# Narrow y groups copied out of PSUM by ScalarE and scaled later by VectorE, and exponentials that stand back from the third query split on, in a two-layer decoder trunk

## The chip, the cores and the metric

The kernel runs on one core of one Trainium2 chip. The metric is the device time of one execution in microseconds (us), the median of several runs. A profile is one further execution, taken with the hardware profiler; its span reaches from the first to the last instruction.

The engines go by the profile's names. PE is the matmul engine and PEld its weight load, ACT is ScalarE, DVE is VectorE, POOL is GpSimd, SP issues most of the DMAs. PSUM is the memory that PE writes its results to, eight banks of 128 x 512 fp32; SBUF is the working memory.

## The reference

One sequence of 256 tokens, width 2048, passes a recurrent layer and an attention layer, each followed by a SwiGLU block:

```
h = rms_norm(x, g);  y_branch, x_branch = split(h @ w_in)        # recurrent block
xb = causal_depthwise_conv(x_branch);  hs = rg_lru(xb)           # gates, a scan over time
x = x + (hs * gelu(y_branch)) @ w_out
x = x + (silu(gate) * up) @ w_out2                               # SwiGLU of rms_norm(x)
k, v = split(rms_norm(x) @ w_kv)                                 # one K/V, k normed by head
q = rms_norm over each head of (rms_norm(x) @ w_q)               # 32 heads of 64, 4 K/V heads
x = x + softmax([mask(q k / 8), sink])[:-1] v @ w_o              # window of 128 tokens
x = x + (silu(gate) * up) @ w_out3
```

All of it is float32.

## The kernel before, in words

**Layout.** Features lie on the partitions, tokens on the free axis: an activation tile is 128 features x 256 tokens, and there are 16 of them. Every operand of a matmul is split into a high part, rounded by an ACT copy, and a low part, the difference, made by DVE. A product is the sum of three matmuls: high weight by high activation, high weight by low activation, low weight by high activation. An activation's two parts lie side by side in one tile of 512 columns.

**Jobs.** The weights come as 707 jobs of 512 KB. `stream` (L278) goes through them: load of job i+4 by SP, split of job i+3 into `hi` and `lo` (L264, L267), matmuls of job i (L330). A group is eight or more jobs that make four output tiles, one bank each (`group`, L347). A bank is wide when the high weight meets both parts of the activation in one matmul of 512 columns, so that two halves have to be added at the end; it is narrow when all three products are added up in 256 columns. With `sync` given, the first two of a group's four banks are wide (L368), without it all four are narrow. At the group's end `done` empties the banks; a bank is handed out again in the order in which it became free.

**The order of the background work.** All else (norms, gates, softmax) is written as generators in a list, `bg`. A job has two half-ticks, each of 12 matmuls of 256 columns. At each, `run_bg` (L203) lets the first generator of the list that is due go on, then the next, until the estimated cost of what it issued passes a budget for DVE (640 ns, later 740) or for ACT (800 ns, later 900); every call through `a`, `tt`, `stt` and `ts` adds its estimate. A plain `yield` leaves a generator due at once, `yield n` puts it off by n half-ticks. If a job's activation isn't there yet, `need` (L216) steps all generators until it is. What is issued in this order is then put in order for each engine by the compiler.

**The recurrent layer** is made in the order x0 x1 x2 g0 x3 g1 y0 g2 g3 y1 g4 g5 y2 g6 g7 y3 (L54): four x groups, eight gate jobs, four y groups. `y_group` (L716) empties its banks through `scaled` (L583), which multiplies by `rstd`, the norm's factor, on the way out of PSUM, into half tiles named h. Its task then computes the gelu, multiplies by the recurrence's result and splits the product into the tiles `zs`, which the groups of `lru_out` consume, two per job. y1 and y3 are given `SYNC`, y0 and y2 are not (L756).

**The attention layer.** Four groups of w_q make 16 tiles q, of two heads each. A group's task (L1012) squares and splits its four tiles (L1020 to L1023), then lets PE sum the squares by head (L1031), copies the sums to a half tile h (L1034), lets PE transpose it (L1039) and makes the heads' factors. `pairs()` (L946) works on the 16 tiles in visits that are three half-ticks apart: a visit issues on PE the values of one tile, the scores of a newer one and the transposes of one between. `softmax` (L910) is a part of it: two masked maxima by DVE (L918), then the Exps by ACT (L934), then a division by POOL. The flag `summing` keeps a softmax from issuing its Exps ahead of the copy L1034. `hold` keeps visits out of the last job of one w_q group and the first of the next.

Of the kernel before, what the change touches and what calls it, by code (L numbers as in the profile page):

```python
# [15 lines left out]
ALU = mybir.AluOpType  # L16
# [3 lines left out]
T = 256  # L20
# [29 lines left out]
class Trunk:  # L50
# [548 lines left out]
    def lru(self, gains, rn):  # L599
# [116 lines left out]
        def y_group(g):  # L716
            def done(ps):
                v = []
                for f in range(4):
                    o = self.half()  # L720
                    self.scaled(o, ps[f])
                    v.append(o)

                def task():
                    th = []
                    yield 1
                    for f in range(4):
                        s = self.slot(F32)
                        o = s[:, 0:T]
                        th.append((s, o))  # L730
                        self.a(o, v[f], AF.Square, scale=math.sqrt(0.044715 * GK))
                        yield
                    for f in range(4):
                        o = th[f][1]
                        self.stt(o, o, GK, v[f], ALU.add, ALU.mult)
                        self.a(o, o, AF.Tanh)
                        yield
                    for f in range(4):
                        s, o = th[f]
                        k = 4 * g + f  # L740
                        self.stt(o, o, 1.0, v[f], ALU.add, ALU.mult)
                        while not hs[k].ready:
                            yield 1
                        h = hs[k].ap[:, 0:T]
                        self.stt(o, o, 0.5, h, ALU.mult, ALU.mult)
                        yield
                        q = self.slot()
                        self.split_act(q, o)
                        self.free(s)
                        self.free(hs[k].ap)  # L750
                        self.free_half(v[f])
                        zs[k].ap = q
                        zs[k].ready = True
                        yield
                self.spawn(task())
            self.group(lambda c: w[g, c], ND, xs, done, g == 3, self.SYNC if g in (1, 3) else ())  # L756

        for step in self.ORDER.split():
# [109 lines left out]
    def attn(self, xs, r, gains, rn):  # L868
# [41 lines left out]
        def softmax(k, rr, ps, sc):  # L910
            f = k % 4
            sm = self.half()
            mx, nm, es, den = (sm[:, 4 * i:4 * i + 4] for i in range(4))
            for hh in range(2):
                for b, c0, c1 in blocks:
                    i = b * 2 + hh
                    self.dve += 69 + 1.042 * (c1 - c0)
                    nc.vector.tensor_tensor_reduce(  # L918
                        sc[hh][:, c0:c1], ps[hh][:, c0:c1], con[:, K_MASK + c0:K_MASK + c1],
                        rr[:, b * 8 + f * 2 + hh:b * 8 + f * 2 + hh + 1],  # L920
                        par[:, C_SINK + 4 * k + hh:C_SINK + 4 * k + hh + 1], ALU.add, ALU.max,
                        accum_out=mx[:, i:i + 1])
                self.free_mbank(ps[hh])
                yield
            while self.summing:
                yield 1
            self.ts(nm, mx, -1.0, None, ALU.mult)
            self.tt(es, par[:, C_SINK + 4 * k:C_SINK + 4 * k + 4], mx, ALU.subtract)
            self.a(es, es, AF.Exp)
            for hh in range(2):  # L930
                for b, c0, c1 in blocks:
                    i = b * 2 + hh
                    o = sc[hh][:, c0:c1]
                    self.a(o, o, AF.Exp, bias=nm[:, i:i + 1], accum_out=den[:, i:i + 1])  # L934
                yield
            self.tt(den, den, es, ALU.add)
            self.rcp(den, den)
            for hh in range(2):
                o = sc[hh][:, P:2 * P]
                nc.gpsimd.tensor_tensor(o, o, sc[hh][:, 2 * P:3 * P], ALU.add)  # L940
                o = sc[hh][:, 0:2 * P].rearrange("p (b q) -> p b q", b=2)
                nc.gpsimd.tensor_tensor(o, o, den[:, hh:4:2].unsqueeze(2).broadcast_to([P, 2, P]), ALU.mult)
                yield
            self.free_half(sm)

        def pairs():  # L946
# [4 lines left out]
            while n < ND or A or B or C:  # L951
# [44 lines left out]
                if new:  # L996
                    sc = [self.slot(F32) for _ in range(2)]
                    yield from softmax(new[0], new[2], ps, sc)
                    C = (new[0], sc)
# [4 lines left out]
        for g in range(4):  # L1004
            def done(ps, g=g):
                v = []
                for p in ps:
                    s = self.slot(F32)
                    self.pull(p, s[:, 0:T])
                    v.append(s)  # L1010

                def task():  # L1012
                    while not self.rv[r].ready:
                        yield 1
                    rt = self.rstd[r][:, T:T + 2]
                    if g == 0:
                        self.stt(r2, rt, 1.0 / HD, rt, ALU.mult, ALU.mult)
                    qs = []
                    for f in range(4):
                        self.a(v[f][:, T:2 * T], v[f][:, 0:T], AF.Square)  # L1020
                        qs.append(self.slot())
                        self.split_act(qs[f], v[f][:, 0:T])
                        yield  # L1023
                    self.summing = True
                    yield 1
                    while not self.room():
                        yield 1
                    p = self.mbank()

                    for f in range(4):  # L1030
                        self.pe_other(p[32 * f:32 * f + 32, 0:T], con[:, K_HS:K_HS + 32], v[f][:, T:2 * T],  # L1031
                                      start=True, stop=True)
                    h = self.half()
                    self.a(h, p[:, 0:T])  # L1034
                    self.summing = False
                    yield
                    yield 1
                    for b in range(2):
                        self.pe_other(p[:, T + b * P:T + b * P + P], h[:, b * P:b * P + P], one, f=nc.tensor.transpose)  # L1039
                    self.free_half(h)  # L1040
                    yield 1
                    rr, m, t = (self.rrs[g][:, 16 * i:16 * i + 16] for i in range(3))
                    for b in range(2):
                        self.ts(m[:, 8 * b:8 * b + 8], p[:, T + b * P:T + b * P + P:16], r2[:, b:b + 1], EPS,
                                ALU.mult, ALU.add)
                    self.free_mbank(p)
                    for q in v:
                        self.free(q)
                    self.rsqrt(rr, m, t)
                    for b in range(2):  # L1050
                        self.ts(rr[:, 8 * b:8 * b + 8], rr[:, 8 * b:8 * b + 8], rt[:, b:b + 1],
                                1.0 / math.sqrt(HD), ALU.mult, ALU.mult)
                    yield
                    for f in range(4):
                        todo.append((4 * g + f, qs[f], rr))
                    if g == 0:
                        self.spawn(pairs())
                    yield
                self.spawn(task())
            self.group(lambda c, g=g: w[g, c], ND, xs, done, g == 3, self.SYNC, packed=True)  # L1060
        self.project(self.d["w_o"], ND, at, gains, rn, late=True)
# [99 lines left out]
```

## Time and profile before

| | |
|---|---|
| runs | 1980.66, 1982.5, 1982.1 us; median 1982.1 us |
| profiled execution | 1980.68 us; span 1978.9 us |
| PE busy | 1971.8 us, 100% of the span |
| DVE busy | 1256.3 us, 63% |
| ACT busy | 1063.0 us, 54% |
| POOL busy | 70.5 us, 4% |
| granted clock of PE | 1.000 |
| DMA | 377.10 MB, mean 191 GB/s |

Busy times are shares of the span and overlap. The end of a matmul is modelled, so a busy PE can hide short waits; they are seen better in the distance from one matmul's start to the next one's. The page divides the span into 40 slices; in tenths, DVE is busy 8988876 in the first seven, that is during the recurrent layer, and 4 to 7 later; ACT 7798655 there, and 3 to 7 later.

### The profile page before, as it was taken

The numbers are of one execution on the slowest core, as the hardware profiler recorded it, in microseconds if no ns is written. First come the engines' busy times: TensorE is split into PE (matmuls) and PEld (weight loads), VectorE is DVE, ScalarE is ACT, GpSimd is POOL, SyncE is SP. The second block draws the span as 40 slices with busy tenths as digits, with TensorE's granted clock in tenths as the row PEclk, the third lists the DMA queues.
The fourth block names the chain that finished last, engine by engine and source line by source line (L and its number), as shares of the span: only waits on it lengthen the run. The fifth ranks groups of instructions, "written<-read, shape, count | busy, mean of one in ns | idle before, by whom it ended". The sixth has DMA issues, their size and how long they took to land.

```text
span 1978.9 us, 40162 instructions
## 1 busy us (share of the span) xinstructions
PE 1971.8 (100%) x16683; PEld 1930.5 (98%) x16683; DVE 1256.3 (63%) x1981; ACT 1063.0 (54%) x1606; POOL 70.5 (4%) x100
## 2 busy tenths in 40 slices
PE   9999999999999999999999999999999999999999
PEld 9999999999999999999999889999999999999999
DVE  8988876556556655545668776755655565554443
ACT  7798655444444444434556775544544454443342
POOL 0000000000000000000002461000000000000000
PEclk9999999999999999999999999999999999999999
DMA  8555655655556555555655335555565556666663
GB/s 289 185 180 189 212 190 190 197 194 192 192 194 195 196 192 193 192 195 196 195 183 180 130 128 168 190 196 192 192 193 196 196 190 196 193 195 204 208 205 126
DMA packets 106198, 377.10 MB, mean 191 GB/s; under 512 B 11936, under 2 KB 14368, under 8 KB 106016
## 3 DMA queue, kind: packets, MB, share of 16 engines
q1 hardware_dynamic: 105408, 373.88, 57.7%
q8 instruction: 130, 2.13, 0.4%
q10 hardware_dynamic: 608, 0.66, 0.1%
q14 instruction: 52, 0.43, 0.1%
HBM read 371.88 MB, written 2.10 MB: 189 GB/s over the span
## 4 chain that ended last, share of the span: by engine, by line
PE 97%; ACT 1%; DVE 1%; issue 0%; POOL 0%; DMA 0%; ACTq 0%; POOLq 0%
PE b L330 93%; PE b L341 1%; PE b L664 1%; ACT s L116 1%; PE b L338 1%; PE b L850 1%; DVE lo L267 0%; ACT hi L264 0%; DVE s L918 0%; PE b L859 0%; PE b L860 0%; PE b L861 0%; DMA x<-in_x 0%; DVE s L125 0%; DVE s L129 0%
## 5 line engine op out<-in xcount | busy, mean ns | idle before, releaser
L330 PE MATMUL b<-s,hi 128*128 128x256 f32 (+1 forms) x10329 | 1432.1, 284 | 1.1 <-DVE h L125 0.6
L330 PEld LDWEIGHTS b<-s,hi 128*128 128x128 f32 x10329 | 1316.8, 188 | 30.5 <-ACT s L116 1.2
L267 DVE TENSOR_TENSOR lo<-raw,hi 128x1024 fp32r<-128x1024 f32 (+1 forms) x707 | 861.5, 1220 | 655.0 <-ACT hi L264 652.6
L264 ACT ACTIVATE hi<-raw 128x1024 fp32r<-128x1024 f32 (+1 forms) x707 | 746.1, 1056 | 808.6 <-PE b L330 750.7
L330 PE MATMUL b<-s,lo 128*128 128x256 f32 x5504 | 827.9, 276 | 0.0
L330 PEld LDWEIGHTS b<-s,lo 128*128 128x128 f32 x5504 | 718.3, 188 | 0.6
L940 POOL TENSOR_TENSOR s<-s 128x128 f32<-128x128 f32 x32 | 14.8, 463 | 1100.4 <-ACT s L116 1097.6
L116 ACT ACTIVATE s<-h 128x256 fp32r<-128x256 f32 (+1 forms) x106 | 40.7, 411 | 23.5 <-DVE h L125 23.5
L116 ACT ACTIVATE t<-b 128x256 f32<-128x256 f32 x130 | 47.9, 375 | 4.1 <-PE b L330 1.7
L116 ACT ACTIVATE s<-x,par 128x256 fp32r<-128x256 f32 x80 | 38.9, 499 | 20.4 <-DVE x L125 13.7
L116 ACT ACTIVATE s<-s 128x256 f32<-128x256 f32 (+2 forms) x116 | 41.7, 412 | 10.9 <-DVE s L129 7.5
L116 ACT ACTIVATE h<-h 128x256 f32<-128x256 f32 (+1 forms) x104 | 38.9, 376 | 3.7 <-DVE h L125 1.5
L116 ACT ACT_TABLE_LOAD x30 | 38.5, 1283 | 0.6
L129 DVE SCALAR_TENSOR_TENSOR s<-x,par,s 128x256 fp32r<-128x256 f32 x80 | 37.6, 479 | 1.8 <-ACT s L116 1.2
L125 DVE TENSOR_TENSOR x<-x,b 128x256 f32<-128x256 f32 x64 | 24.1, 415 | 21.2 <-PE b L330 21.2
L125 DVE TENSOR_TENSOR h<-b,rstd 128x256 f32<-128x256 f32 x100 | 37.5, 414 | 0.0
L125 DVE TENSOR_TENSOR h<-h,rstd 128x256 f32<-128x256 f32 x94 | 35.3, 416 | 0.0
L125 DVE TENSOR_TENSOR s<-s,s 128x256 fp32r<-128x256 f32 (+2 forms) x84 | 32.4, 416 | 4.1 <-ACT s L116 4.0
L125 DVE TENSOR_TENSOR h<-h,h 128x256 f32<-128x256 f32 x88 | 34.7, 415 | 0.5 <-ACT h L116 0.5
L125 DVE TENSOR_TENSOR s<-h,s 128x256 fp32r<-128x256 f32 x88 | 34.9, 417 | 0.1
L125 DVE TENSOR_TENSOR h<-b,t 128x256 f32<-128x256 f32 x92 | 34.5, 415 | 0.0
L116 ACT ACTIVATE s<-s,h 128x128 f32<-128x128 f32 x64 | 28.2, 442 | 10.2 <-DVE h L134 5.2
(99 smaller groups left out, 612.0 us busy)
## 6 DMA issues: line engine op xcount, KB each, us to landing
raw<-in_ffn_in SPq DMA_DIRECT2D x352, 512.0 KB, 3.4
raw<-in_ffn_out SPq DMA_DIRECT2D x176, 512.0 KB, 3.5
raw<-in_lru_in SPq DMA_DIRECT2D x62, 512.0 KB, 3.8
raw<-in_lru_out SPq DMA_DIRECT2D x32, 512.0 KB, 4.1
raw<-in_w_q SPq DMA_DIRECT2D x32, 512.0 KB, 3.4
raw<-in_w_o SPq DMA_DIRECT2D x32, 512.0 KB, 3.3
raw<-in_gate SPq DMA_DIRECT2D x8, 512.0 KB, 3.7
raw<-in_kv SPq DMA_DIRECT2D x8, 512.0 KB, 4.3
```

The costliest lines, as they stand in the source:

```text
L116: self.nc.scalar.activation(out, in_, func, **kw)
L125: self.nc.vector.tensor_tensor(out, a, b, op)
L129: self.nc.vector.scalar_tensor_tensor(out, a, s, b, op0, op1)
L264: high = self.ins(self.nc.scalar.activation(hi[:, q], raw[:, q], AF.Copy))
L267: self.nc.vector.tensor_tensor(lo[:, q], raw[:, q], hi[:, q].bitcast(F32), ALU.subtract)
L330: self.nc.tensor.matmul(*args, **kw)
L338: self.other = self.ins(f(*args, **kw))
L341: self.other = self.ins(f(*args, **kw))
L664: nc.tensor.matmul(out[j], (hi if high else lo)[:, c:c + P], x2[kt][:, q:q + T], start=kt == 0 and high > q, stop=kt == 1 and not high)
L850: nc.tensor.matmul(ps[f][:, 0:T], w0, x2[kt][:, q:q + T], start=k0 + kt == 0 and high > q, stop=k0 + kt == ND - 1 and not high)
L940: nc.gpsimd.tensor_tensor(o, o, sc[hh][:, 2 * P:3 * P], ALU.add)
```

## The change

In `y_group`, a group whose first bank is narrow has its four banks copied to the half tiles by `pull` without a factor, which is an ACT copy (L414). The multiplication by `rstd` is done at the start of the task, in the half tiles, with a plain yield after each. Groups with wide banks go on as before. In `softmax`, every Exp first waits for `summing` to be false. In a w_q group's task the flag is set at the third split, where it was set after the yield behind the fourth.

```diff
         def y_group(g):
             def done(ps):
                 v = []
+                plain = not ps[0][1]
                 for f in range(4):
                     o = self.half()
-                    self.scaled(o, ps[f])
+                    if plain:
+                        self.pull(ps[f], o)
+                    else:
+                        self.scaled(o, ps[f])
                     v.append(o)
 
                 def task():
                     th = []
                     yield 1
+                    if plain:
+                        for o in v:
+                            self.tt(o, o, self.rstd[0][:, 0:T], ALU.mult)
+                            yield
                     for f in range(4):
...
                 for b, c0, c1 in blocks:
                     i = b * 2 + hh
                     o = sc[hh][:, c0:c1]
+                    while self.summing:
+                        yield 1
                     self.a(o, o, AF.Exp, bias=nm[:, i:i + 1], accum_out=den[:, i:i + 1])
...
                         qs.append(self.slot())
                         self.split_act(qs[f], v[f][:, 0:T])
+                        self.summing = f > 1
                         yield
-                    self.summing = True
                     yield 1
```

## The prediction

> **What bounds the kernel now.** I read the page's busy times and chain first, then the waits, then the timeline around the few waits that end on PE.
>
> ```profile
> span 1978.9 us, 40162 instructions
> PE 1971.8 (100%) x16683; PEld 1930.5 (98%) x16683; DVE 1256.3 (63%) x1981; ACT 1063.0 (54%) x1606; POOL 70.5 (4%) x100
> PE 97%; ACT 1%; DVE 1%; issue 0%; POOL 0%; DMA 0%; ACTq 0%; POOLq 0%
> ...
> PE b L338 <- ACT h L116: 1.2, 1, 1.2
> ...
> PE b L330 <- DVE h L125: 0.6, 2, 0.4
> PEld b L330 <- DVE h L125: 0.6, 1, 0.6
> ```
>
> PE is the whole kernel: it is busy for 1971.8 of 1978.9 us and holds 97% of the chain. The change adds no matmul and removes none, so it can gain only what PE loses by waiting, and lose only by making PE wait. The two waits shown are where its edits aim: PE waits for DVE on h tiles (0.6 us in two pieces) and once, 1.2 us, for an ACT copy named h.
>
> The first of them is the start of y3, at 181 us. The rows: PE's timeline (start and length in us, the idle time before in brackets), one piece of the chain in order of time for PE's pace, and DVE's timeline.
>
> ```profile
> 180.92 0.28 PE L664 MATMUL b<-s,lo 128*128 128x256 f32 x1
> 181.49 0.47 PE L330 MATMUL b<-s,hi 128*128 128x256 f32 x2 [0.29 <-DVE h L125]
> 182.31 0.98 PE L330 MATMUL b<-s,hi 128*128 128x256 f32 x6 [0.35 <-DVE h L125]
> ...
> 99.58 21.76 PE b L330 x192
> ...
> 179.93 0.74 DVE L125 TENSOR_TENSOR h<-b,rstd 128x256 f32<-128x256 f32 x2
> 180.59 0.41 DVE L125 TENSOR_TENSOR s<-s,s 128x256 f32<-128x256 f32 x1
> 180.93 0.41 DVE L125 TENSOR_TENSOR h<-b,rstd 128x256 f32<-128x256 f32 x1
> 181.26 0.68 DVE L709 TENSOR_TENSOR_SCAN s<-s,s 128x256 f32<-128x256 f32 x1
> 181.86 0.39 DVE L125 TENSOR_TENSOR h<-b,rstd 128x256 f32<-128x256 f32 x1
> ```
>
> The row of 192 matmuls gives PE's pace, 21.76 / 192 = 0.113 us each. Three matmuls start from 180.92 up to the one at 182.31; they need 0.34 us and take 1.39, so PE loses 1.05 us there. What it waits for is DVE's last two h<-b,rstd: they empty y2's third and fourth bank, and y3, which takes over y2's four banks, begins with its two narrow ones. y2's matmuls had ended two gate jobs (2 x 24 x 0.113 = 5.4 us) earlier. DVE is simply late.
>
> **The change, part by part.** *Edit 1, the y groups in narrow banks.* Only y0 and y2 are built without SYNC (L756), so only they have `ps[0][1]` false. Each drops four DVE multiplies out of PSUM, gains four ACT copies out of PSUM, and gets its four multiplies back in the task, SBUF to SBUF. The rows: the tile rstd's instructions on DVE up to 215 us, two groups of the lines by form (busy us, mean ns), ACT's timeline.
>
> ```profile
> L125 DVE TENSOR_TENSOR h<-b,rstd x12: 394/414/418, 120.6 to 211.8; 128x256 f32<-128x256 f32 x12
> ...
> L116 ACT ACTIVATE t<-b 128x256 f32<-128x256 f32 x130 | 47.9, 375 | 4.1 <-PE b L330 1.7
> ...
> L125 DVE TENSOR_TENSOR h<-h,rstd 128x256 f32<-128x256 f32 x94 | 35.3, 416 | 0.0
> ...
> 178.39 1.01 ACT L116 ACTIVATE s<-s 128x256 f32<-128x256 f32 x3
> 180.44 0.72 ACT L116 ACTIVATE s<-h 128x256 f32<-128x256 f32 x2 [1.03 <-DVE h L125]
> ```
>
> Twelve such multiplies lie between 120.6 and 211.8 us: four of y0, four of y2, two each of y1 and y3. Eight go, 8 x 414 ns, and eight come, 8 x 416 ns: DVE's sum stays. ACT gains 8 x 375 ns = 3.0 us, 1.5 in each group. The second of y2's two 0.75 us halves fits into the 1.03 us that ACT now idles at 179.4, waiting for the very multiplies that go. Since PE ended y2 at 175.8, the copies can run between 176 and 180, before y3 asks for the banks at 181.03 (180.92 + 0.113). So the loss at y3's start goes: **-1.05 us**, or nothing, if the copies land behind 182.
>
> [...]
>
> What is late next? y2's chain (square, tanh, the product with h, the split into zs) now starts behind a copy and a multiply, and the planner's ACT budget, charged with 4 x 313 ns more at y2's end, holds the recurrence back by about three half-ticks (my walk through L203 to L210 from there). DVE and ACT have little air in the following stretch. The rows: three windows (length, then PE, PEld, DVE and ACT busy), then DVE's and PE's timeline.
>
> ```profile
> 175.80:182.30 6.50, 5.87 (x50) 5.50 (x48) 6.47 (x14) 5.44 (x11) 0.00 (x0) 1.00 0.65 204
> 182.30:203.90 21.60, 21.59 (x176) 21.20 (x177) 20.05 (x40) 21.51 (x42) 0.00 (x0) 1.00 0.53 180
> 203.90:223.00 19.10, 19.10 (x162) 18.73 (x161) 19.10 (x39) 14.69 (x27) 0.00 (x0) 1.00 0.52 171
> ...
> 218.86 0.75 DVE L125 TENSOR_TENSOR s<-s,s 128x256 fp32r<-128x256 f32 x2
> ...
> 221.34 0.75 DVE L125 TENSOR_TENSOR s<-s,s 128x256 fp32r<-128x256 f32 x2
> 222.01 3.49 DVE L267 TENSOR_TENSOR lo<-raw,hi 128x1024 fp32r<-128x1024 f32 x3
> ...
> 222.63 1.30 PE L330 MATMUL b<-s,hi 128*128 128x256 f32 x10
> ```
>
> ACT is full during y3 (21.51 of 21.60) and DVE is full during the first group of lru_out (19.10 of 19.10). The work that closes this stretch is the split of zs14 and zs15, DVE's pair at 221.34 to 222.09. lru_out's eighth job takes zs14 with the ninth matmul of the last row, 222.63 + 8 x 0.113 = 223.53, and zs15 three matmuls later. So the slack is 1.8 us, and with PE 1.05 us earlier it is 0.75. DVE's sum is unchanged, so its end moves only by idle time that the later start of the chain tears into it; I take up to 0.75 us of that as free, and 0.1 us as lost (a first wait of the seventh job, whose zs12 and zs13 have 1.5 us of slack now). Edit 1: -0.95 us, between -1.05 and the price of rival B.
>
> *Edits 2 and 3, the exponentials.* A test in the loop at L931 and the flag set at the third split instead of after the fourth issue no instruction. They matter only where a softmax stands between its maximum (L918) and its last Exp while a query group is between its third split and its sums. At the four group ends pairs() is held (`self.hold`, L961) until the second job of the next group, so no softmax is open when the splits run: the splits come, then the visit with its scores, and its softmax reaches L925 one half-tick later, with the flag already set in both versions. The sums and the copy L1034 are issued in that half-tick, the flag falls, and the Exps follow in the next. By my walk the order of issue stays as it is at all four ends. The rows: PE's and ACT's timeline at the fourth end, then ACT's at the third.
>
> ```profile
> 1157.88 0.40 PE L338 MATMUL b<-s,con 128*32 128x256 f32 x1
> ...
> 1158.44 1.63 PE L330 MATMUL b<-s,hi 128*128 128x256 f32 x12
> 1161.29 0.33 PE L338 MATMUL b<-con,h 128*128 128x128 f32 x1 [1.21 <-ACT h L116]
> ...
> 1160.38 0.40 ACT L116 ACTIVATE s<-s,h 128x128 f32<-128x128 f32 x1 [1.73 <-DVE h L134]
> ...
> 1160.87 0.36 ACT L116 ACTIVATE h<-b 128x256 f32<-128x256 f32 x1
> ...
> 1126.35 0.36 ACT L116 ACTIVATE h<-b 128x256 f32<-128x256 f32 x1
> 1127.16 0.21 ACT L116 ACTIVATE h<-h 128x4 f32<-128x4 f32 x1 [0.45 <-DVE h L125]
> ```
>
> The sums are done at 1158.5, but an Exp that waits 1.73 us for DVE's negated maximum stands ahead of the copy on ACT; PE's transposes lose 1.21 us. At the third group (1126.35) the copy runs ahead of the Exps and PE loses nothing. Since the planner issues both alike, the difference was made by the compiler's ordering behind it, which the flag does not reach. [...] I take 0 for edits 2 and 3; the ends are -1.2 us (the copy comes first) and +1.36 us (a visit slips by a half-tick, 12 x 0.113, with nothing to cover it; behind a held softmax stand pairs() and its next visit, on ACT nothing).
>
> **Sum.** -0.95 + 0 = about -0.9 us: span 1978.0. The profiled execution took 1980.68 us, 1.8 more than its span, and the median of the three runs, 1982.1, lies 1.4 above it. So 1982.1 - 0.9 = **1981.2 us**.
>
> **The rivals.**
> A. *The stand-back works after all*: some softmax is caught, or the compiler orders the copy first now. Then the 1.21 us of the fourth group go too: 1982.1 - 0.9 - 1.2 = 1980.0. For it: the wait has just this shape. Against it: the walk finds no softmax that the new test stops.
> B. *The y chain becomes the bound, and the kernel is slower.* Place: lru_out's seventh and eighth job, 220 to 224 us. The four multiplies and copies push zs14 and zs15 back; the three lo splits that now run behind them (3.49 us) may go ahead of them. From a delay of 0.75 us it eats into the gain, from 1.8 us it makes the kernel slower. A 1.5 us delay (ACT's four copies in the full stretch) gives 1981.8; the full 3.5 us gives 1982.1 + 1.7 = 1983.8. For it: both windows are full, and my walk has the chain later. Against it: DVE's work is the same, and ACT idles 1.03 us where the copies fall.
> C. *Edit 1 does not empty the banks sooner*: ACT is put on the copies behind its table load and the squares, and y3 waits as now: 1982.1.
>
> **How the numbers follow.** Forecast 0.53, A 0.15, B 0.22, C 0.10. The forecast's own range is 1980.3 to 1982.0, which holds the runs' own spread (1980.66 to 1982.5 before). With A below and most of B above, the range is 1979.3 to 1984.0. Differences of 0.2% (4 us) are about what a measurement of this kernel can tell from no change. The stalls that the change can reach add up to 2.3 us, so faster by more needs something that the profile does not show: 0.04. B reaches it only with a second stall of the same size elsewhere, for instance where held visits leave w_o short of its inputs: 0.07. Within: 0.89.
>
> **What would show it.** Right: four h<-b,rstd left of twelve, eight more h<-h,rstd, eight ACT copies h<-b; no DVE wait before y3's first matmuls; and PE still waiting some 1.2 us for ACT's h near 1160. Wrong: that last wait gone (A); PE waiting at 219 to 224 for an s tile of DVE or ACT (B); y3 still waiting, now for ACT h (C). A change of the number of matmuls, or of visits' spacing in the attention stretch, would overturn the walk for edits 2 and 3.

## The result, and the profile after

| | before | after |
|---|---|---|
| median of 20 runs each, taken together | 1980.88 us (1980.12 to 1983.23) | 1984.59 us (1983.3 to 1986.13) |
| profiled execution; span | 1980.68; 1978.9 us | 1983.46; 1981.7 us |

The ratio is 1.0016, with a 95% interval of 1.001 to 1.0022: the change makes the kernel 2.0 to 4.4 us slower, around 3.2. The forecast was 1981.2 us; 1984.59 lies 0.6 us above the upper end of its range. The runs of each kernel fall into two groups about 1.8 us apart, and in all twelve profiled executions the group goes with the form of the start (the last section), so a median moves with their mixture; the two compared here are of the same group and differ by 2.8 us. That is the difference to explain.

From the page of the kernel after (busy times, the chain's shares, two groups), then its waits that end on PE (us in total, times, longest):

```profile
PE 1974.5 (100%) x16683; PEld 1932.7 (98%) x16683; DVE 1256.5 (63%) x1981; ACT 1066.1 (54%) x1614; POOL 70.5 (4%) x100
...
PE 92%; ACT 3%; DVE 3%; issue 1%; POOL 0%; DMA 0%; ACTq 0%; DVEq 0%; POOLq 0%
...
L125 DVE TENSOR_TENSOR h<-h,rstd 128x256 f32<-128x256 f32 x102 | 38.5, 417 | 0.0
...
L125 DVE TENSOR_TENSOR h<-b,rstd 128x256 f32<-128x256 f32 x92 | 34.3, 414 | 0.0
```

```profile
PE b L338 <- ACT h L116: 1.2, 1, 1.2
...
PE b L330 <- ACT s L116: 0.6, 2, 0.4
PE b L330 <- DVE s L125: 0.6, 1, 0.6
...
PEld b L330 <- ACT hi L264: 0.3, 1, 0.3
```

Edit 1 is there: eight multiplies out of PSUM fewer, eight in SBUF more (102 for 94), eight ACT copies more (1614 for 1606 instructions). The wait for DVE's h at y3's start is gone, ACT's h at 1162 us is waited for as before, and there are new waits, for s tiles of DVE (0.6 us) and ACT (0.6, of which 0.4 is the execution's start). But PE's *busy* time grew too, by 2.7 us with the same 16683 matmuls, and its waits don't account for that. So the waits alone don't answer; the two traces have to be laid over each other, matmul by matmul. The figures below are the start of the same matmul in a kernel less its start in the kernel before, in us, with what they differ by at 150 us (the start of the execution) taken off. The experiments are in the same table.

```
matmul at (before, us)     by 150 | 180.9  182.5  187.1    190    202    209    220  224.6    232   1165   1200   1970
after                        0.00 |  1.05  -0.09  -0.08   0.24   0.62   0.88   0.93   2.71   2.84   2.83   2.83   2.83
e1  edits 2 and 3 alone     -0.42 |  0.00   0.04  -0.06  -0.16  -0.41  -0.41   0.20   0.38   0.51   0.50   0.50   0.50
e2  edit 1 in y0 alone      -0.32 |  1.07   0.19   0.19   0.19   0.19   0.19   0.19   0.19   0.19   0.17   0.17   0.17
e3  edit 1 in y2 alone       0.23 |  0.00  -0.78  -0.78   0.09   0.47   0.71   1.07   2.55   2.83   2.80   2.80   2.80
e4  no multiplies            1.63 |  0.00  -1.00  -1.10  -0.84  -0.46  -0.17   0.46   0.46   0.46   0.42   0.42   0.42
e6  banks turned             0.19 |  0.00  -1.16  -1.31  -0.95  -0.75  -0.49   0.09   0.09   0.09   0.05   0.05   0.05
e7  copy first               1.83 |  0.00  -0.03  -0.03  -0.03  -0.03  -0.03  -0.03  -0.03  -0.03  -1.49  -0.69  -0.69
e8  y2 alone, uncharged      1.66 |  0.00  -0.83  -0.83  -0.03   0.39   0.39   1.18   3.45   3.73   3.70   3.70   3.70
e9  y2 alone, at once       -0.14 |  0.00  -0.25  -0.25  -0.25  -0.19   0.06   0.42   0.63   0.76   0.74   0.74   0.74
e10 y2 alone, copies first   1.51 |  0.00  -1.16  -1.31   2.02   2.47   2.64   2.63   2.63   2.63   2.61   2.61   2.61
```

All of the change's 2.83 us arises between 154 and 232 us; the attention stretch adds nothing. There are four pieces.

**154 to 181: +1.05, with no wait.** PE's timeline before and after, the same eight matmuls early in y2:

```profile
155.65 1.07 PE L330 MATMUL b<-s,lo 128*128 128x256 f32 x8
```

```profile
155.70 1.10 PE L330 MATMUL b<-s,lo 128*128 128x256 f32 x8
```

Take off the last one's own 0.28 us and divide by the seven distances: 0.113 us before, 0.117 after. PE runs at a slower pace, and it keeps it: by the starts of the trace it is 117.7 ns against 113.3 up to 181 us and beyond. It began with one distance of 129 ns, from 154.51 to 154.64, where y2's matmuls reach its fourth bank: the load of the first weight for that bank waits for DVE, which empties the bank for y1, 0.18 us later than before. DVE's last pair of y1, before and after:

```profile
153.44 0.75 DVE L125 TENSOR_TENSOR h<-b,rstd 128x256 f32<-128x256 f32 x2
```

```profile
153.62 0.74 DVE L125 TENSOR_TENSOR h<-b,rstd 128x256 f32<-128x256 f32 x2
```

This is y0's part of edit 1 at work: with y2 alone changed (e3) the slow pace doesn't come, with y0 alone (e2) it does. It is the moved multiplies rather than the copies, for with the copies and without the multiplies (e4) it doesn't come either.

**181 to 187: -1.13.** y3 starts without a wait, 0.11 us behind the last gate's matmul:

```profile
181.97 0.28 PE L664 MATMUL b<-s,lo 128*128 128x256 f32 x1
182.08 1.10 PE L330 MATMUL b<-s,hi 128*128 128x256 f32 x8
```

That is the gain foreseen, and it only makes up for the slower pace. The copies free the last bank at 181.62 us where the multiplies did at 182.25, 0.6 us sooner; that no wait at all is left is also due to PE's coming later. With y2 alone (e3), where PE comes on time, 0.78 of the 1.05 us goes.

**187 to 220: +1.0.** PE waits for a weight's high half from ACT (the PEld row above; from 187.61 the next matmul starts 0.22 us late) and is at the slow pace until 211.65 us, where it was back at the fast one from 197.22 before.

**220 to 232: +1.9.** PE waits twice for zs15, the last of the products: at 225.54 for its high half, which ACT makes, at 226.57 for its low half, which DVE makes. PE's timeline, then DVE's (the splits of zs14 and zs15, each behind a weight's low half):

```profile
225.00 0.28 PE L330 MATMUL b<-s,lo 128*128 128x256 f32 x1
225.54 0.39 PE L330 MATMUL b<-s,hi 128*128 128x256 f32 x1 [0.27 <-ACT s L116]
226.57 0.39 PE L330 MATMUL b<-s,hi 128*128 128x256 f32 x1 [0.64 <-DVE s L125]
```

```profile
223.15 1.22 DVE L267 TENSOR_TENSOR lo<-raw,hi 128x1024 fp32r<-128x1024 f32 x1
224.29 0.42 DVE L125 TENSOR_TENSOR s<-s,s 128x256 fp32r<-128x256 f32 x1
...
224.96 1.22 DVE L267 TENSOR_TENSOR lo<-raw,hi 128x1024 fp32r<-128x1024 f32 x1
226.09 0.42 DVE L125 TENSOR_TENSOR s<-s,s 128x256 fp32r<-128x256 f32 x1
```

zs15 is split by 226.51, where the pair at 221.34 ended at 222.09: 4.42 us later. zs14 and zs15 belong to y3 (`k = 4 * g + f` in `y_group`), which the change leaves as it was, and y3's own chain begins on time: DVE has emptied its banks by 212.24 us (212.18 before). What has moved is the last recurrence's work, whose scans y3's products need (`hs[k]`). Before, DVE did all four of these scans ahead of emptying y3's banks; after, three of them and one product come behind. DVE's timeline before (the last two scans, y3's last two banks), then after (the banks, two scans, the product, the last scan):

```profile
207.80 1.27 DVE L709 TENSOR_TENSOR_SCAN s<-s,s 128x256 f32<-128x256 f32 x2
...
211.43 0.74 DVE L125 TENSOR_TENSOR h<-b,rstd 128x256 f32<-128x256 f32 x2
```

```profile
211.50 0.74 DVE L125 TENSOR_TENSOR h<-b,rstd 128x256 f32<-128x256 f32 x2
...
213.30 1.26 DVE L709 TENSOR_TENSOR_SCAN s<-s,s 128x256 f32<-128x256 f32 x2
...
215.59 0.42 DVE L125 TENSOR_TENSOR s<-s,s 128x256 f32<-128x256 f32 x1
...
216.26 0.68 DVE L709 TENSOR_TENSOR_SCAN s<-s,s 128x256 f32<-128x256 f32 x1
```

From there to zs15's split DVE also works off two more of the weights' low halves than before (six for four). Three scans of 0.6 us, a product of 0.4 and two low halves of 1.2 are the 4.4 us, for DVE has next to no idle time in this stretch. The delay arises 45 us earlier, as ACT's timeline after and DVE's multiplies after show:

```profile
178.57 1.02 ACT L116 ACTIVATE s<-s 128x256 f32<-128x256 f32 x3
179.49 0.91 ACT L116 ACTIVATE h<-b 128x256 f32<-128x256 f32 x3
180.29 1.06 ACT L264 ACTIVATE hi<-raw 128x1024 fp32r<-128x1024 f32 x1
181.24 0.38 ACT L116 ACTIVATE h<-b 128x256 f32<-128x256 f32 x1
182.74 0.42 ACT L116 ACTIVATE s<-h 128x256 f32<-128x256 f32 x1 [1.11 <-DVE h L125]
183.65 0.42 ACT L116 ACTIVATE s<-h 128x256 f32<-128x256 f32 x1 [0.50 <-DVE h L125]
...
193.39 0.71 ACT L116 ACTIVATE s<-h 128x256 f32<-128x256 f32 x2
```

```profile
182.28 0.42 DVE L125 TENSOR_TENSOR h<-h,rstd 128x256 f32<-128x256 f32 x1
...
183.22 0.40 DVE L125 TENSOR_TENSOR h<-h,rstd 128x256 f32<-128x256 f32 x1
...
184.67 0.75 DVE L125 TENSOR_TENSOR h<-h,rstd 128x256 f32<-128x256 f32 x2
```

The copies stand behind three of an earlier recurrence's four Sqrts, the multiplies come at 182.28 to 185.4, and so y2's four squares (s<-h) are torn: two at 182.74 and 183.65, the other two at 193.39, behind eight sigmoids of the gates and two table loads. Before, they came in two pairs, at 180.44 and here:

```profile
182.02 0.71 ACT L116 ACTIVATE s<-h 128x256 f32<-128x256 f32 x2
```

The gelu of half of y2 thus starts 11 us later, and from 175.8 us to zs15's split DVE idles 3.17 us in all, where it idled 1.58.

### The profile page after: what moved, and what is told of

It reads as the page before. It is cut to its first block, busy times and chain, and to the rows that moved or that the text cites. A ratio compares the mean times of both kernels' runs of the same rounds, so it can differ in the third digit from the quotient of the medians.

```text
span 1981.7 us, 40166 instructions
## 1 busy us (share of the span) xinstructions
PE 1974.5 (100%) x16683; PEld 1932.7 (98%) x16683; DVE 1256.5 (63%) x1981; ACT 1066.1 (54%) x1614; POOL 70.5 (4%) x100
## 4 chain that ended last, share of the span: by engine, by line
PE 92%; ACT 3%; DVE 3%; issue 1%; POOL 0%; DMA 0%; ACTq 0%; DVEq 0%; POOLq 0%
PE b L330 89%; ACT s L116 2%; DVE lo L267 1%; PE b L341 1%; ACT hi L264 1%; PE b L338 1%; ACT L116 1%; PE b L858 1%; DVE s L129 1%; DVE s L125 0%; PE b L664 0%; DVE s L926 0%; DVE s L709 0%; DVE h L125 0%; PE b L867 0%
```

## The experiments

The theory after the result: **y2's chain** (copy, multiply, square) is late because its parts stand late in the engines' queues, and it pushes back the work that stands behind it there, up to the last zs. Rivals: the flag (edits 2 and 3); y0; the planner's ACT budget, which the copies charge; the copies themselves; and a step more in a full stretch, wherever it stands.

**e1: edits 2 and 3 alone.** The second and third hunk of the change on the kernel before.

> The two edits on the exponentials alone (the test in the loop and the flag at the third split); the y groups as before. Theory: these edits change no order of instructions, so the time is that of the kernel before within 0.5 us, and PE still loses 1.2 us on ACT's h at the fourth group's transposes. Rival (the held exponentials cost the 2.8 us): at least 2 us slower, with visits of the attention stretch further apart than 36 columns of matmuls.

Measured 1982.32 us (before 1981.45), ratio 1.0002, interval 0.9993 to 1.0011. The compiled program is that of before, instruction for instruction on each engine. These edits do nothing, as predicted. It is also a measure of the table: the same program, profiled twice, differs by up to 0.5 us between 150 and 232 us. Differences below that are not read.

**e2 and e3: edit 1 in y0 alone, in y2 alone.**

```diff
-                plain = not ps[0][1]
+                plain = g == 0          # e3: g == 2
```

> Only y0 is copied by ACT and scaled later; y2 as before. Theory: y0's multiplies make DVE some 0.2 us later at y1's pulls, y2's fourth bank comes a few hundredths of a us late near 154.5 us, PE falls from 113 to 118 ns per narrow matmul there and stays so up to the next run of wide matmuls, 1.0 us by 181 us. That eats the wait at y3's start (1.05 us before), so the sum is 0 to +0.5 us against before. Rival (y0's part is free): PE stays at 113 ns through y2 and the time is that of before, with the full wait at y3's start.

Measured 1981.1 us, ratio 0.9998 (0.9989 to 1.0007). y0 costs nothing, though it alone brings the slow pace of 154 to 181 us (+1.07 in the table): the wait at y3's start, still there in this kernel, shrinks by most of it (0.19 is left in the table). So 0.88 of the 1.07 us that PE had lost ahead of this wait cost nothing here.

> Only y2 is copied by ACT and scaled later; y0 as before. Theory: no loss of pace at 154.5 us; the wait at y3's start shrinks from 1.05 us to at most 0.5; but zs14 and zs15 come late and PE waits 1 to 1.5 us near 225 us, so the sum is +0.5 to +2 us against before. Rival (the whole loss comes from y0's part): about 1 us faster than before and no wait near 225 us.

Measured 1983.67 us, ratio 1.0012 (1.0003 to 1.0021). y2 alone carries the whole cost, with no slow pace ahead of 181 us. In the profiled execution it is 2.80 us, more than the 2 foreseen. Two of its waits on PE:

```profile
PE b L330 <- DVE s L125: 0.6, 1, 0.6
PE b L330 <- ACT hi L264: 0.6, 1, 0.6
```

They are new, at 226 and 187 us.

**e4: the change without its eight multiplies.** y0 and y2 stay unscaled in this kernel.

```diff
                     yield 1
-                    if plain:
-                        for o in v:
-                            self.tt(o, o, self.rstd[0][:, 0:T], ALU.mult)
-                            yield
```

> The changed kernel without the eight late multiplies: y0 and y2 stay unscaled, that part of the computation is left out. DVE has 8 x 0.33 us less to do, ACT the same copies. Theory: what makes the change slow is DVE's later chain, so the hitch at 154.5 us and the wait near 225 us go, and the time is 0.5 to 1.5 us below before. Rival (ACT's copies are the cost, by their place in ACT's queue): still 1.5 to 3 us above before, with the wait near 225 us.

Measured 1982.57 us, ratio 1.0002 (0.9993 to 1.0011): neither the gain of 0.5 us foreseen nor the rival's loss of 1.5. PE does not wait at 225 us. DVE's last pair of splits:

```profile
223.31 0.75 DVE L125 TENSOR_TENSOR s<-s,s 128x256 fp32r<-128x256 f32 x2
```

It ends at 224.06; less the 1.63 us by which this execution started late, that is 222.43, 0.3 us behind the kernel before. So the copies alone don't make it late; the multiplies are needed for that. This kernel also spares DVE their time; whether it is the time or the place, e9 tests. One of y2's four squares is torn off here too (at 193.93), so a torn square alone does not make zs15 late. And the copies alone gain nothing in the end: the 1.0 us of y3's start is given back by 220 us in distances between matmuls that are 0.1 to 0.3 us too long, at places where a weight's high or low half has only just been made, and in pace.

**e8: y2 alone, with the planner's budgets charged as before.** The copies' ACT estimate is taken back in `done`, DVE is charged there with the four multiplies, and the multiplies in the task, all four issued at once there, charge nothing. The edit against e3, cut:

```diff
+                if plain:
+                    self.act -= 4 * (100 + 0.833 * T)
+                    self.dve += 4 * (69 + 1.042 * T)
...
-                            self.tt(o, o, self.rstd[0][:, 0:T], ALU.mult)
-                            yield
+                            self.nc.vector.tensor_tensor(o, o, self.rstd[0][:, 0:T], ALU.mult)
```

> Only y2 is copied by ACT and scaled later, but the planner's budgets are charged as if DVE had emptied the banks, and the four multiplies are issued with y2's first square, uncharged. Theory A (the budget, charged on ACT, holds the recurrence back, and that makes zs15 late): no wait above 0.3 us near 225 us, and 0.5 to 1 us faster than before. Theory B (the copies themselves, in ACT's queue, and the multiplies behind them are what makes it late): the waits near 187 and 225 us stay, and the time is 2 to 3 us above before, as with y2 alone.

Measured 1984.6 us (before 1981.79), ratio 1.0016 (1.0007 to 1.0025). With the budgets as before the loss is, if anything, larger, so what the copies charge isn't the cause; zs15's split comes later still:

```profile
228.51 0.41 DVE L125 TENSOR_TENSOR s<-s,s 128x256 fp32r<-128x256 f32 x1
```

**e9: y2 alone, the multiplies issued straight behind the copies.** The edit against e3, cut:

```diff
                     v.append(o)
+                if plain:
+                    for o in v:
+                        self.tt(o, o, self.rstd[0][:, 0:T], ALU.mult)
                 def task():
...
-                    if plain:
-                        for o in v:
-                            self.tt(o, o, self.rstd[0][:, 0:T], ALU.mult)
-                            yield
```

> Narrow copies for y2 alone, with the four multiplies issued straight behind the copies instead of in the task some ticks later. Theory B (the y chain is late because its parts stand late in the queues: the multiplies at 182 to 185 us, and two of y2's four squares only at 193, behind the gates' sigmoids and two table loads): three squares now stand with the copies ahead of the sigmoids, the chain of y2 closes earlier, PE's two waits near 225 us (0.44 and 0.91 with y2 alone) fall to 0.5 us or less in all; the time is within 0.7 us of before. The rival (the copy and the multiply as an added step in a full stretch cost what they cost, wherever they stand): the waits near 225 us stay over 1 us, the time 1.5 to 3 us above before.

Measured 1982.98 us (before 1981.36), ratio 1.0005 (0.9997 to 1.0014). ACT's last square of y2 (the other three end by 183.12), then DVE's last two splits:

```profile
192.44 0.40 ACT L116 ACTIVATE s<-h 128x256 f32<-128x256 f32 x1
```

```profile
221.85 0.43 DVE L125 TENSOR_TENSOR s<-s,s 128x256 fp32r<-128x256 f32 x1
...
223.66 0.42 DVE L125 TENSOR_TENSOR s<-s,s 128x256 fp32r<-128x256 f32 x1
```

Same instructions, another place: three squares in time instead of two, one scan of the recurrence behind y3's banks instead of three, zs15 by 224.08 instead of 226.51, no wait at 225. In the profiled execution 0.74 us over before are left of 2.80, at the edge of the 0.7 foreseen; the interval holds zero. The rival, that the added step costs its 1.5 to 3 us wherever it stands, is out; up to the 0.74 it may cost something.

**e10: y2 alone, the Sqrts put behind y2's last copy.** The edit, cut; `self.copied` is set by y2's last copy:

```diff
+            behind, self.copied = self.copied, None
+            with ExitStack() as after:
+                if behind is not None:
+                    after.enter_context(self.tc.issue_after(behind))
-            for k, r, i in v:
-                self.a(A(r), A(r), AF.Sqrt, scale=-1.0)
+                for k, r, i in v:
+                    self.a(A(r), A(r), AF.Sqrt, scale=-1.0)
```

> Narrow copies for y2 alone, with the recurrence's four Sqrts put behind y2's last copy on ACT; the multiplies in the task as in the change. If the place of the copies behind the three Sqrts is what makes y2's chain late: the copies end some 1.5 us earlier, by 180 us, PE does not wait at y3's start, the waits near 225 us fall to 0.5 us or less, time within 0.7 us of before. If it is the tearing of the squares (two of the four are still issued behind the gates' sigmoids and a table load here, as with y2 alone): the waits near 225 us stay at 1 us or more and the time is 1.5 to 3 us above before; the Sqrts' own delay can add to it at the recurrence's next products.

Measured 1984.77 us, ratio 1.0013 (1.0004 to 1.0022). Neither expectation fits whole. The squares stay torn (two at 197.29), and zs15 is 4.2 us late as with y2 alone, so the Sqrts ahead of the copies were not the cause. Yet PE doesn't wait at 225, because a new wait has made PE late itself: ACT has a table load of 1.28 us ahead of the Sqrts, now in the midst, and another between them and the gates' sigmoids (183.45 and 186.11 us), and the weights' split stands behind both (188.84).

```profile
189.97 2.75 PE L331 MATMUL b<-s,hi 128*128 128x256 f32 x11 [1.81 <-ACT hi L265]
```

**e6: y3's first two banks given to its narrow tiles** (on the kernel before), a way to remove the wait at y3's start with no copy; `turned` is given to y3 alone.

```diff
+                        if turned:
+                            ps = ps[2:] + ps[:2]
```

> The kernel before, where y3 gives the first two banks that it gets to its narrow matmuls and the last two to its wide ones, which come 1.4 us later; nothing else is changed. Theory: the 1.05 us wait at y3's start goes, and with it the slow pace behind it (up to 0.6 us): 1 to 1.6 us faster. Rival (DVE's chain behind it is the bound, so that what is gained at y3 is lost near 223 us): the wait goes, but a wait for zs14 or zs15 of 0.5 to 1 us comes, and the sum is within 0.5 us.

Measured 1980.89 us (before 1981.79), ratio 0.9998 (0.999 to 1.0007). The wait goes (-1.16), and by 220 us all of it is given back at the same kind of places (188, 201 and 213 us), not at zs14 or zs15, where the rival had put it; the 1 to 1.6 us foreseen don't come. The 1.05 us that the prediction put down as a gain is not kept by any of the ways tried: DVE and ACT are right behind PE here.

**e7: the Exps put behind the copy L1034** (on the kernel before), what edits 2 and 3 would have done had they reached the compiler. The edit, cut:

```diff
+            behind, self.copied = self.copied, None
...
+                with ExitStack() as after:
+                    if behind is not None:
+                        after.enter_context(self.tc.issue_after(behind))
...
+                        self.a(o, o, AF.Exp, bias=nm[:, i:i + 1], accum_out=den[:, i:i + 1])
...
+                    self.copied = self.ins(nc.scalar.activation(h, p[:, 0:T], AF.Copy))
```

> The kernel before, with the Exps of the softmax that follows a head sum put behind the copy of the sums on ACT. Theory: this is what the flag could not do; the 1.2 us wait of PE for ACT's h near 1161 us goes, and nothing else: 1.2 us faster. Rival (the wait only moves, to the next visit's values): PE waits as long at the visit near 1164 or 1171 us, and the time is that of before.

Measured 1980.5 us, ratio 0.9997 (0.9989 to 1.0006). ACT's timeline (the copy, and the first Exp behind it) and the first row of the waits on PE:

```profile
1160.36 0.39 ACT L1041 ACTIVATE h<-b 128x256 f32<-128x256 f32 x1
1162.21 0.21 ACT L117 ACTIVATE h<-h 128x4 f32<-128x4 f32 x1 [1.46 <-DVE h L126]
```

```profile
PE b L339 <- POOL s L990: 1.0, 2, 0.7
```

The wait for ACT's h is gone (-1.46 in the table from 232 to 1165 us), and 0.8 of it comes back at 1197 us, later than the rival had it, where PE now waits 0.7 us for POOL's division. Some 0.7 us are left, which these runs can't tell from zero. No version here beats the kernel before by more than its interval.

**e5: PE's pace.** The kernel before, with no wide banks in 22 groups of the second layer's first SwiGLU product: the same arithmetic in matmuls of 256 columns alone.

```diff
-            self.group(lambda c, g=g: w[g, c], ND, xs, done, g == NH // 2 - 1, self.SYNC)
+            self.group(lambda c, g=g: w[g, c], ND, xs, done, g == NH // 2 - 1, () if l else self.SYNC)
```

> The kernel before, with SYNC taken from the 22 groups of the second layer's first FFN product, so that their 176 jobs have no run of wide matmuls. Theory of the two paces (a hitch puts PE from 113.3 to 117.7 ns per narrow matmul, and only a run of wide matmuls brings it back): PE falls at the norm's sums near 1270 us and stays at 117.7 ns to the end of those groups, some 479 us later: about 18 us slower. Rival (PE recovers by itself after some 15 to 20 us): within 1 us of before.

Measured 2000.15 us (before 1981.79), ratio 1.0093 (1.0079 to 1.0107). The chain in order of time (start, us, count):

```profile
1259.92 12.24 PE b L330 x108
1272.16 0.43 PE b L338 x2
1272.60 527.44 PE b L330 x4479
```

12.24 / 108 = 0.1133 us a matmul; behind the two short ones of a norm 527.44 / 4479 = 0.1178, for the rest of the piece, with no wait in it. By the starts of the trace the slow pace lasts to 1762.35 us, behind the third run of wide matmuls that comes again. 490 us at 0.0044 / 0.1177 more make 18.3 us; the medians differ by 18.4, the two traces by 18.0 over these groups.

## Why the prediction was wrong

**The bound, and edits 2 and 3: right.** PE bounds both kernels. The flag reached no instruction (e1), and the 1.2 us wait was the compiler's order: putting the copy first by force (e7) removes it. Rival A is out: nothing was caught. In e7, with the Exps queued behind it, the copy runs at 1160.36, and it is the Exp that waits 1.46 us for DVE.

**Edit 1's removed term, -1.05: right as a mechanism, worth nothing.** Rival C is out: the copies end by 181.62, y3 doesn't wait, and in e3 and e4, where PE comes on time, the wait shrinks by 0.78 and 1.0 us. But PE came to that place 1.05 us later by its slower pace, which no step of the prediction had, so that the wait's going altogether is in part luck; and where PE comes on time (e4, e6) the gain is given back by 220 us.

**The cost of the moved multiplies: right.** 417 ns in SBUF, 414 out of PSUM. DVE's busy sum stayed (1256.5 for 1256.3 us).

**The step that failed: "DVE's sum is unchanged, so its end moves only by idle time that the later start of the chain tears into it; I take up to 0.75 us of that as free, and 0.1 us as lost".** The end, zs15's split, moved by 4.42 us. The sum did stay, but it says nothing of where in the queue the instructions stand, and the end moved by order too, not by idle time alone. The added idle time is 1.6 us, twice what was taken as free; all of it lies ahead of y3's banks, so that some 2 us of the recurrence's work was left for behind them, and two more low halves, 2.4 us, went ahead of the split as well. The prediction had said that the recurrence would be held back, by about three half-ticks or 4.1 us, but gave this no term: y3's products need its scans, and these came up to 7.9 us later, behind y3's banks (216.26 for 208.40). The program issues the copies at y2's end and the multiplies in the task; in the trace each multiply starts 2.8 to 4.7 us behind its copy, and half of the squares come behind the next gates' sigmoids. e9 moves the multiplies and the yields between them, nothing else, and loses 0.74 instead of 2.80 us. The charge on the ACT budget that the prediction named as the reason for the delay is not it (e8).

**Rival B was the case, and its price too low.** Place (zs14 and zs15 in lru_out) and point of decision (1.8 us) were right, and the point can be tested on six kernels. Lateness of zs15's split against 222.09, less the column "by 150"; lateness of PE at 220 us; what the slack of 1.8 us then leaves as a wait; and what PE lost from 220 to 224.6:

```
           zs15    PE    zs15 - PE - 1.8    lost
after      4.42   0.93        1.69          1.78
e3         4.26   1.07        1.39          1.48
e8         5.17   1.18        2.19          2.27
e9         2.13   0.42       -0.09          0.21
e4         0.34   0.46       -1.92          0.00
e10        4.18   2.63       -0.25          0.00
```

The rule holds to 0.1 us, but for a small loss with e9, where it is at its edge. What was wrong was the top of the delay: 3.49 us, three low halves that might go ahead. It was 4.42: two low halves, and the recurrence's scans and product, for which B had no term. The same six kernels show it. Lateness of the emptying of y3's banks; what DVE then does ahead of zs15's split; and the time from the one to the other:

```
         emptying   scans  products  low halves    to zs15's split
before       0.00       0         0           4               9.91
after        0.06       3         1           6              14.27
e3          -0.09       3         1           6              14.26
e8           1.07       2         2           6              14.01
e9           0.08       1         1           5              11.96
e4           0.35       0         0           4               9.91
e10         -0.97       3         3           6              15.06
```

The emptying's lateness and the time above 9.91 add up to the column zs15 in each. And the wait is only 1.8 of B's cost: the 1.0 us between 187 and 220 (a wait for ACT's high half, and the pace) lay outside every rival. Why the compiler's order tears the squares at two in the change and at three in e9, and by which link y2's late chain puts the recurrence behind y3's banks, is open.

**The range.** Its upper end was B's top price, 1983.8. With 4.42 for 3.49 alone it would have been 1984.7. The base was off too, the other way: 1982.1, the median of three runs, lies 1.2 us above that of the 20.

## What to carry to other kernels

Moved to another memory at the same price (417 ns for 414), the multiplies were not free here, with PE 2.83 us later in the end. For such a move ask where the new place lies in each queue, and what the next step of the chain will stand behind there; the sum of busy time can't show it. Slack (the consumer's start less the producer's end) held to 0.1 us on five of six kernels and was the most reliable number here; a delay has to be walked through the queues, instruction by instruction, before it is set against it. A wait on PE ahead of a stretch in which other engines are full was mostly a loan here: remove it, and look where PE arrives too early next (e4, e6, e7).

## What the runs showed of the hardware

**PE showed two paces at one granted clock:** 113.3 and 117.7 ns per matmul of 256 columns, with the clock at 1.00 in every window of both that was read. In the kernel after PE fell into the slower behind a single start 16 ns late (129 ns for 113, 154.64 us). The way back was mostly a run of three matmuls of 512 columns: by the starts in the kernel before, 12 of 17 returns stand directly behind such a run, and 26 of the 38 such runs met at the slow pace did not end it; the other five returns are in the making of k and v (four, 1015 to 1034 us) and at 1158.67 us, behind the short matmuls of a head sum. e5 without such runs stayed slow for 490 us, at a price of 18.4 us. What the second pace is, was not found out.

**Behind a wait of 1.81 us the clock was at half.** Windows of e10 (length, PE, PEld, DVE, ACT and POOL busy, granted clock, DMA share, GB/s):

```profile
190.00:191.00 1.00, 1.00 (x4) 0.83 (x5) 1.00 (x1) 1.00 (x4) 0.00 (x0) 0.86 0.00 0
191.00:192.00 1.00, 1.00 (x6) 0.98 (x5) 0.84 (x3) 1.00 (x3) 0.00 (x0) 0.50 0.00 0
192.00:193.00 1.00, 1.00 (x7) 1.00 (x6) 0.65 (x1) 1.00 (x2) 0.00 (x0) 0.50 0.78 225
193.00:194.00 1.00, 1.00 (x6) 1.00 (x6) 1.00 (x2) 0.98 (x2) 0.00 (x0) 0.50 0.77 299
194.00:195.00 1.00, 1.00 (x9) 1.00 (x9) 0.71 (x1) 0.99 (x3) 0.00 (x0) 0.93 0.48 107
```

From the means, the clock was at half for 0.28 + 3 + 0.14 = 3.4 us; by the trace's own record from 190.72 to 194.14 us, 0.7 us behind the wait's end. Half of that, 1.7 us as an estimate, is lost, most of it (1.4) ahead of the matmul in the table's column 190, and with the wait of 1.8 that makes up nearly all of the 3.3 us by which e10 falls back there from 187.1. The mean clock is 0.999 in eight of e10's eleven runs and 1.000 in all runs of the other kernels; half the clock for 3.4 of 1983 us makes 0.999, so by this estimate the dip comes in most executions, not in all. The record of the full clock lasts 1972.904 us before and 1976.317 us after: 3.413 us more, about the length of the dip, and 578 and 579 times that. Whether the wait is what halved the clock was not tested. The wait of 1.2 us near 1160 left the clock at 1.00, before and after.

**The start of an execution has two forms.** PE's first matmuls of the first product in the kernel before, and in e10:

```profile
7.05 1.10 PE L330 MATMUL b<-s,hi 128*128 128x256 f32 x8
```

```profile
8.49 1.70 PE L331 MATMUL b<-s,hi 128*128 128x256 f32 x8
```

In five of the twelve profiles (e4, e5, e7, e8, e10) the first matmuls come 0.21 us apart for some 4 us, as in e10's stretch at half clock (eight starts from 192.51 to 194.19 us), and the execution is 1.5 to 1.8 us late by 150 us (those in the table); in the other seven the slow start is shorter. The windows show the clock as 1.00 there, but the trace's record of it only begins later: at 9.3 to 10.6 us in those five, where the 0.21 us end, and at 4.1 to 7.0 us in the seven. That the clock is still at half there is an estimate from the 0.21 us alone; no record shows it.
